# Two accumulators of the four-output stages from another PSUM pool, the first norm's factor later, the output in four stores

## The chip, the cores and the metric

One core of a Trainium2 chip runs the whole program. The metric is the device time of one execution in microseconds (us). The core has TensorE (PE in the profile, its weight loads PEld), VectorE (DVE), ScalarE (ACT), GpSimd (POOL) and SyncE (SP); a q behind the name is the engine's instruction queue, where waits and DMA issues stand.

## The reference

Two layers on 256 tokens of width 1024, in float32, batch 1:

```python
for l in range(DEPTH):                       # DEPTH = 2
    h = rms_norm(x, norm_mix_w[l])
    x = x + hybrid_mixer(h, ...)             # attention over 64 chosen keys + a Mamba-2 scan, gated, merged
    h = rms_norm(x, norm_ffn_w[l])
    x = x + conv_glu_ffn(h, ...)             # up to 2 x 2816, causal conv, silu gate, down
return rms_norm(x, norm_final_w)
```

`rms_norm` divides a token by the root of its mean square and multiplies by a weight. `hybrid_mixer` multiplies h by `w_in`: 584 columns with index queries, index keys and head weights, together with 32 columns of time steps, make the 616 "narrow columns"; then come q, k, v, the scan's columns and two gates. The results are projected, gated, added and multiplied by `w_out`.

## The kernel before

Activations stand transposed in SBUF: 8 tiles of 128 features by 256 tokens (`xT`). Every float32 product is made of three fp32r products: high part of the weights by high part of the input, high by low, low by high. The weights come in 512 KB chunks through SP's queue into 5 buffers (`raw`); ACT casts a chunk to its high part (`whi`, L199), DVE subtracts to get the low part (`wlo`, L200), into 3 pairs of buffers. Some chunks are split long ahead into SBUF tiles that are free just then (names with an e in front: `es`, `ez`, `ex`, `eths`, `eXt`, `ebig`, `ehxh`, `ehxl`). `take()` hands the next chunk to the products.

PSUM has 8 banks, each a tile: 4 with the tag `acc` (sums of the big products), 2 with `sa` (attention and half of the narrow columns), 2 with `sb` (norms and scan). Two helpers make the big products:

- `n_outer` makes one tile of 128 outputs, over all inputs, in one `acc` bank: 16 high products (L376, L377) and 8 low ones (L382) for each chunk.
- `k_outer` makes four tiles of outputs at once in four banks, input by input, so that it can start before its last inputs are there. There are four of these stages in a layer: the scan's projection (inputs `bH`), `w_out` (`mH`), FFN up (`uh`) and FFN down (`fH`). In each the four outputs come first and `n_outer` makes the others.

The tiles are emptied by DVE or ACT: `merge` (L841), `residual` (L857, adds to `xT`, then makes the next norm's inputs `uh`, `ul` and squares `sq`), `times_factor` (L891).

The norm's factor is not needed by the products: sums of squares collect in `ssq` on POOL (L343), `factor()` adds them over features with 8 small TensorE products against ones (L361), takes the power -0.5 on POOL (`ny`, L282), and, one step later, spreads it to a row (L289, L290, L298, L300). `factor()` is a side task: it is registered with a delay, counted in chunks taken, and its instructions are queued on TensorE behind the last low product emitted until then (`issue_after(st["mm"].ins)`).

```python
side("norm", nrm.factor(), 7)      # first norm of the program
side("norm", nrm.factor(), 2)      # in the w_out stage, for the FFN's norm
```

The first norm's factor so comes when the eighth and last narrow chunk (k = 7) is taken. The narrow columns take two `acc` and two `sa` banks; their eviction by ACT (L570 to L572) multiplies by the factor.

The order on each engine is not the program's: a planner replays it on modelled times and lays each engine's instructions out in a fixed order, in which each then waits for its semaphores. Weight splits, and the norm's steps after the small products, have high priority in it.

At the end four transposed tiles of the output (two halves `h` for each of two blocks of tokens `c`) are scaled by the last norm's factor, `h = 0` on ACT (L932), `h = 1` on DVE (L930), and each `c` is stored with one DMA on SP's queue (L933).

Of the kernel before, what the change touches and what calls it, by code (L numbers as in the profile page):

```python
# [18 lines left out]
P = 128  # L19
L = 2  # L20
T = 256
D = 1024
KD = D // P
# [40 lines left out]
def hybrid_kernel(ctx: ExitStack, tc: tile.TileContext, a: dict, out: bass.AP):  # L64
    nc = tc.nc
# [9 lines left out]
    def pst(tag, shape, bufs):  # L75
        t = psum.tile([P, 512], F32, name=tag, tag=tag, bufs=bufs)
        n = int(np.prod(shape[1:]))
        v = t[:shape[0], :n]
        if len(shape) == 3:
            v = v.rearrange("p (a b) -> p a b", a=shape[1])  # L80
        return v
# [61 lines left out]
    def side(lane, gen, delay):  # L143


        lanes[lane].append([st["now"] + delay, gen])

    def side_step(lane):
        q = lanes[lane]
        with tc.issue_after(st["mm"].ins):  # L150
            d = next(q[0][1], None)
        if d is None:
            q.pop(0)
        else:
            q[0][0] = st["now"] + d
# [32 lines left out]
    def take():  # L188
        i = st["cur"]
        with tc.high_priority():  # L190
            load_some()
            while st["prep"] < len(order):
                j = order[st["prep"]]
                if j not in early and sum(k not in early for k in splits) == SPLIT_BUFS:
                    break
                src, b, c = chunks[j]
                hi, lo = (t[:, :b * c] for t in split_tiles(j))
                r = raws.pop(j)
                nc.scalar.copy(out=hi, in_=r)  # L199
                nc.vector.tensor_sub(lo, r, hi.bitcast(F32))  # L200
                splits[j] = [t.rearrange("p (b c) -> p b c", b=b) for t in (hi, lo)]
                st["prep"] += 1
                load_some()
        st["cur"] += 1
        if st["mm"] is not None:
            side_steps()
        return splits.pop(i)
# [29 lines left out]
    def constants():  # L237
        with tc.issue_after(nrm.add.ins):
            nc.gpsimd.dma_start(ident, a["ident"])
            nc.gpsimd.dma_start(small[:, L * KD:], a["small"][:, L * KD:])  # L240
            nc.gpsimd.dma_start(tri, a["tri"])
            nc.gpsimd.dma_start(rope, a["rope"])
            nc.gpsimd.dma_start(cmask, a["cmask"])
        nc.vector.tensor_scalar(neg, cmask, -FILL, FILL, op0=OP.mult, op1=OP.add)
        nc.vector.tensor_scalar(half, small[:, o0:o0 + L * 5 * XT], 0.5, None, op0=OP.mult)

    def sm(name, l=None, n=None):
        o, w = _SMALL[name]
        v = small[:, o:o + w]
        if l is not None:  # L250
            v = v[:, l * (w // L):(l + 1) * (w // L)]
        return v
# [117 lines left out]
    def acc_tile():  # L370
        return pst("acc", [P, T], 4)

    def feed_high(ps, wh, hi, lo, ks, first):

        for j, k in enumerate(ks):
            nc.tensor.matmul(ps, wh[:, j, :], hi(k), start=first and j == 0, stop=False)  # L376
            nc.tensor.matmul(ps, wh[:, j, :], lo(k), start=False, stop=False)  # L377

    def feed_low(ps, wl, hi, ks, last):

        for j, k in enumerate(ks):
            st["mm"] = nc.tensor.matmul(ps, wl[:, j, :], hi(k), start=False, stop=last and j == len(ks) - 1)  # L382

    def k_outer(n_pairs, hi, lo):

        pss = [acc_tile() for _ in range(4)]
        for j in range(n_pairs):
            wh, wl = (w.rearrange("p (k n) c -> p k n c", k=2) for w in take())
            for kk in range(2):
                for n in range(4):  # L390
                    feed_high(pss[n], wh[:, kk, n:n + 1, :], hi, lo, [2 * j + kk], j == 0 and kk == 0)
            for n in range(4):
                feed_low(pss[n], wl[:, :, n, :], hi, [2 * j, 2 * j + 1], j == n_pairs - 1)
        return pss
# [9 lines left out]


    nrm = Normed(sm("nmw", 0))
    side("norm", nrm.factor(), 7)

    for l in range(L):

# [132 lines left out]
        def wide(pss, ws, hi, lo, first, last):  # L543

            halves = [slice(t * P, (t + 1) * P) for t in range(2)]
            for t, s in enumerate(halves):
                for ps, w in zip(pss[t], ws):
                    nc.tensor.matmul(ps, hi[:, s], w[0], start=first, stop=False)  # L548
            for t, s in enumerate(halves):
                for ps, w in zip(pss[t], ws):  # L550
                    nc.tensor.matmul(ps, lo[:, s], w[0], start=False, stop=False)  # L551
            for t, s in enumerate(halves):
                for ps, w in zip(pss[t], ws):
                    st["mm"] = nc.tensor.matmul(ps, hi[:, s], w[1], start=False, stop=last)  # L554

        pss = [[pst("acc", [P, 308], 4), pst("sa", [P, 308], 2)] for _ in range(2)]
        for k in range(KD):
            if l == 0:
                nrm.parts(k)
                for i in ([k - 1] if k < KD - 1 else [k - 1, k]):  # L560
                    if i >= 0:
                        nrm.square(i)
                if k == 3:
                    constants()
            wh, wl = take()
            ws = [(wh[:, 0, o:o + 308], wl[:, 0, o:o + 308]) for o in (0, 308)]
            wide(pss, ws, nrm.hi(k), nrm.lo(k), k == 0, k == KD - 1)
        for t in range(2):
            r = nrm.cols[:, t:t + 1]
            nc.scalar.activation(tok[t][:, 308:576], pss[t][1][:, 0:268], AF.Copy, scale=r)  # L570
            nc.scalar.activation(wd[:, t, :], pss[t][1][:, 268:308], AF.Copy, scale=r)
            nc.scalar.activation(tok[t][:, 0:308], pss[t][0], AF.Copy, scale=r)  # L572
# [3 lines left out]
        for c in range(2, 5):  # L576
            pss = [pst("acc", [P, 512], 4) for _ in range(2)]
# [6 lines left out]
            for t in range(2):  # L584
# [4 lines left out]
                else:  # L589
                    o = 576 + (c - 3) * 512  # L590
# [222 lines left out]
        for g in range(4):  # L813
            finish("scan", 3 - g)
            y = xs[g]
            for i in range(4):
# [6 lines left out]
                if i == 0:  # L823
                    acc = tmp.tile([P, T], F32, name="ssq", tag="ssq", bufs=3)
# [21 lines left out]
        for n, ps in enumerate(k_outer(8, bh, bl)):  # L846
            merge(n, ps)
# [6 lines left out]
        nrm = Normed(sm("nfw", l))  # L854
# [5 lines left out]
        for n, ps in enumerate(k_outer(4, mh, ml)):  # L860
            residual(n, ps, 0.5)
# [27 lines left out]
        def times_factor(ps):  # L889
            t = tmp.tile([P, T], F32, name="cu", tag="cu", bufs=4)  # L890
            nc.vector.tensor_mul(t, ps, nrm.row)  # L891
            return t

        pss = k_outer(4, nrm.hi, nrm.lo)
        finish("norm")
        us = [times_factor(ps) for ps in pss]
# [14 lines left out]
        nrm = Normed(sm("nlw") if last else sm("nmw", l + 1), not last)  # L911
# [9 lines left out]
    y = act.tile([P, 2, 2, 512], F32, name="y", tag="hxl")  # L921
    for c in range(2):
        for h in range(2):
            ps = pst("acc", [P, 512], 4)
            for i in range(4):
                nc.tensor.transpose(ps[:, i * P:(i + 1) * P], nrm.xw[:, 4 * h + i, c * P:(c + 1) * P], ident)
            o = y[:, c, h, :]
            r = nrm.cols[:, c:c + 1]
            if h:
                nc.vector.tensor_scalar(o, ps, r, None, op0=OP.mult)  # L930
            else:
                nc.scalar.activation(o, ps, AF.Copy, scale=r)  # L932
        nc.sync.dma_start(out[c * P:(c + 1) * P, :], y[:, c].rearrange("p a b -> p (a b)"))  # L933

# [81 lines left out]
```

## Time and profile before

| | |
|---|---|
| device time, 3 runs | 1081.49, 1083.02, 1076.52 us; median 1081.49 us |
| the profiled execution | 1080.03 us, its span 1078.2 us |
| granted TensorE clock, mean | 0.998 |
| PE, DVE, ACT, POOL busy | 1062.6, 862.8, 694.0, 81.7 us |
| TensorE products | 8713 |
| bytes moved by DMA | 191.84 MB, mean 178 GB/s |

The span runs from the first to the last instruction; 1.83 us of the execution's time lie around it. A product is shown from its issue to a modelled end, 0.28 us for 256 columns, although the next one starts 0.12 us later; so the busy time of TensorE is not its load, and an idle time shown before a product is 0.16 us shorter than the stop.

### The profile page before, as it was taken

The page shows a single profiled execution, that of the slowest core. Times are in us where ns is not written, and L with a number is a line of the kernel's source. Part 1 is how long each engine was busy: PE and PEld are TensorE (multiplying, and loading weights), DVE is VectorE, ACT ScalarE, POOL GpSimd, SP SyncE. Part 2 cuts the span into 40 slices and gives each one's busy share as a digit, 9 for nine tenths or more (in the row PEclk, how much of TensorE's full clock was granted, in tenths as well). Part 3 has the DMA queues.
Part 4 walks back from the last instruction along what each step waited for, and adds up shares of the span by engine and source line. Part 5 has one row for each costly group of instructions (what it writes and reads, how often), then busy time and mean ns, then how long its engine had stood idle before and what let it go on. Part 6 is the DMA issues. An engine that isn't in the chain of part 4 may idle for free.

```text
span 1078.2 us, 22404 instructions
## 1 busy us (share of the span) xinstructions
PE 1062.6 (99%) x8713; PEld 1023.9 (95%) x8713; DVE 862.8 (80%) x1652; ACT 694.0 (64%) x1285; POOL 81.7 (8%) x86
## 2 busy tenths in 40 slices
PE   8999999999999999999999999999999999999997
PEld 7789998999999999999997999999999999999997
DVE  6999987979776898886577999887895878988642
ACT  6758887657555566665455788875674555666552
POOL 3000000024000100000100000000420020000010
PEclk9999999999999999999999999999999999999999
DMA  8646544555677346667645654455567761666661
GB/s 303 189 149 206 156 157 145 168 167 179 193 238 238 102 138 196 195 190 232 186 136 175 218 167 126 164 165 161 178 181 220 247 213 40 195 195 192 187 182 50
DMA packets 53530, 191.84 MB, mean 178 GB/s; under 512 B 6144, under 2 KB 7184, under 8 KB 52400
## 3 DMA queue, kind: packets, MB, share of 16 engines
q1 hardware_dynamic: 51840, 181.23, 54.4%
q0 software_dynamic: 1440, 9.16, 2.3%
q8 instruction: 69, 1.13, 0.4%
q14 instruction: 37, 0.30, 0.1%
q10 hardware_dynamic: 144, 0.01, 0.0%
HBM read 189.26 MB, written 1.11 MB: 177 GB/s over the span
## 4 chain that ended last, share of the span: by engine, by line
PE 88%; DMA 4%; DVE 3%; issue 2%; ACT 2%; POOL 0%; SPq 0%; POOLq 0%; DVEq 0%; ACTq 0%
PE acc L376 24%; PE acc L377 24%; PE acc L382 24%; PE acc L551 2%; PE acc L554 2%; PE acc L548 2%; DMA raw<-in_wu_dram 2%; PE sb L729 1%; PE sa L613 1%; PE sa L465 1%; DVE wlo L200 1%; PE sa L638 1%; DMA bc<-prd 1%; DVE ul L330 1%; DMA raw<-in_wi_dram 1%
## 5 line engine op out<-in xcount | busy, mean ns | idle before, releaser
L199 ACT CAST whi<-raw 128x1024 fp32r<-128x1024 f32 (+2 forms) x320 | 331.9, 1041 | 227.6 <-PE acc L377 172.8
L200 DVE TENSOR_TENSOR wlo<-raw,whi 128x1024 fp32r<-128x1024 f32 (+2 forms) x320 | 387.4, 1213 | 102.7 <-ACT whi L199 96.0
L376 PE MATMUL acc<-hxh,whi 128*128 128x256 f32 x1456 | 352.5, 282 | 0.0
L377 PE MATMUL acc<-hxl,whi 128*128 128x256 f32 x1456 | 349.7, 280 | 0.0
L377 PEld LDWEIGHTS acc<-hxl,whi 128*128 128x128 f32 x1456 | 274.2, 188 | 2.3 <-issue 2.2
L376 PEld LDWEIGHTS acc<-hxh,whi 128*128 128x128 f32 x1456 | 274.2, 188 | 1.6 <-issue 1.5
L382 PE MATMUL acc<-hxh,wlo 128*128 128x256 f32 x1456 | 202.6, 280 | 0.0
L382 PEld LDWEIGHTS acc<-hxh,wlo 128*128 128x128 f32 x1456 | 182.7, 188 | 0.5 <-issue 0.3
L376 PE MATMUL acc<-fH,whi 128*128 128x256 f32 x352 | 84.4, 279 | 1.3 <-DVE xT L857 1.3
L377 PE MATMUL acc<-fL,whi 128*128 128x256 f32 x352 | 84.2, 279 | 0.0
L673 DVE SCALAR_TENSOR_TENSOR cv<-acc,half,cv 128x255 f32<-128x255 f32 (+2 forms) x144 | 66.9, 473 | 4.2 <-ACT cv L671 3.8
L875 DVE SCALAR_TENSOR_TENSOR cv<-acc,small,cv 128x255 f32<-128x255 f32 (+1 forms) x144 | 68.7, 477 | 1.4
L376 PEld LDWEIGHTS acc<-fH,whi 128*128 128x128 f32 x352 | 66.1, 188 | 1.6 <-issue 1.5
L343 POOL TENSOR_TENSOR ssq<-ssq,sq 128x256 f32<-128x256 f32 x30 | 28.3, 943 | 503.5 <-ACT sq L339 499.3
L377 PEld LDWEIGHTS acc<-fL,whi 128*128 128x128 f32 x352 | 66.0, 188 | 0.0
L376 PE MATMUL acc<-bH,whi 128*128 128x256 f32 x256 | 62.3, 280 | 0.0
L377 PE MATMUL acc<-bL,whi 128*128 128x256 f32 x256 | 62.2, 282 | 0.0
L382 PE MATMUL acc<-fH,wlo 128*128 128x256 f32 x352 | 49.6, 279 | 0.0
L376 PEld LDWEIGHTS acc<-bH,whi 128*128 128x128 f32 x256 | 48.1, 188 | 0.3 <-issue 0.2
L377 PEld LDWEIGHTS acc<-bL,whi 128*128 128x128 f32 x256 | 48.2, 188 | 0.0
L719 ACT ACTIVATE bc<-bc,nP 128x128 f32<-128x128 f32 x128 | 39.8, 391 | 10.3 <-DMA bc<-prd 10.2
L382 PEld LDWEIGHTS acc<-fH,wlo 128*128 128x128 f32 x352 | 44.8, 188 | 0.0
(312 smaller groups left out, 1848.9 us busy)
## 6 DMA issues: line engine op xcount, KB each, us to landing
raw<-in_wu_dram SPq DMA_DIRECT2D x88, 512.0 KB, 4.2
raw<-in_wx_dram SPq DMA_DIRECT2D x48, 512.0 KB, 3.7
raw<-in_wd_dram SPq DMA_DIRECT2D x38, 512.0 KB, 4.3
raw<-in_wz_dram SPq DMA_DIRECT2D x32, 512.0 KB, 3.6
raw<-in_wp_dram SPq DMA_DIRECT2D x32, 512.0 KB, 4.6
raw<-in_wq_dram SPq DMA_DIRECT2D x24, 512.0 KB, 4.3
raw<-in_wgs_dram SPq DMA_DIRECT2D x16, 512.0 KB, 3.6
bc<-prd POOLq DMA_DIRECT2D x8, 1024.0 KB, 7.4
```

The costliest lines, as they stand in the source:

```text
L199: nc.scalar.copy(out=hi, in_=r)
L200: nc.vector.tensor_sub(lo, r, hi.bitcast(F32))
L343: self.add = nc.gpsimd.tensor_add(self.acc, self.acc, sq)
L376: nc.tensor.matmul(ps, wh[:, j, :], hi(k), start=first and j == 0, stop=False)
L377: nc.tensor.matmul(ps, wh[:, j, :], lo(k), start=False, stop=False)
L382: st["mm"] = nc.tensor.matmul(ps, wl[:, j, :], hi(k), start=False, stop=last and j == len(ks) - 1)
L548: nc.tensor.matmul(ps, hi[:, s], w[0], start=first, stop=False)
L551: nc.tensor.matmul(ps, lo[:, s], w[0], start=False, stop=False)
L554: st["mm"] = nc.tensor.matmul(ps, hi[:, s], w[1], start=False, stop=last)
L673: nc.vector.scalar_tensor_tensor(v[:, j:], ps[:, :T - j], cw(l, 3 - j, i), v[:, j:], op0=OP.mult, op1=OP.add)
L719: nc.scalar.activation(E[:, h, :], E[:, h, :], AF.Relu, bias=nP[:, c, 8 * g + h:8 * g + h + 1])
L875: nc.vector.scalar_tensor_tensor(v[:, j:], uu[:, :T - j], fw(l, 2 - j, i), v[:, j:], op0=OP.mult, op1=OP.add)
```

## The change

`k_outer` takes two banks with the tag `acc` and two with `sa`, in that order, instead of four `acc`. The first norm's factor gets a delay of 9 chunks, which is not reached in the narrow stage; instead its first step is emitted right behind the stage's loop, in front of the evictions. Each block of the output is stored in two halves of 128 x 512 numbers, `h = 0` through SP's queue, `h = 1` through POOL's, each as soon as it is scaled.

```diff
     def k_outer(n_pairs, hi, lo):
 
-        pss = [acc_tile() for _ in range(4)]
+        pss = [pst(tag, [P, T], bufs) for tag, bufs in (("acc", 4), ("acc", 4), ("sa", 2), ("sa", 2))]
...
     nrm = Normed(sm("nmw", 0))
-    side("norm", nrm.factor(), 7)
+    side("norm", nrm.factor(), KD + 1)
...
             wide(pss, ws, nrm.hi(k), nrm.lo(k), k == 0, k == KD - 1)
+        if l == 0:
+            side_step("norm")
         for t in range(2):
...
                 nc.scalar.activation(o, ps, AF.Copy, scale=r)
-        nc.sync.dma_start(out[c * P:(c + 1) * P, :], y[:, c].rearrange("p a b -> p (a b)"))
+            (nc.gpsimd if h else nc.sync).dma_start(out[c * P:(c + 1) * P, h * 512:(h + 1) * 512], o)
```

## Rows read from the trace of the kernel before

**Rows 1.** The chain that ended last, shares of the span by engine.

```profile
PE 88%; DMA 4%; DVE 3%; issue 2%; ACT 2%; POOL 0%; SPq 0%; POOLq 0%; DVEq 0%; ACTq 0%
```

**Rows 2.** Waits of PE: waiting line, who ended it, total us, times, longest.

```profile
PE acc L376 <- DVE xT L857: 4.4, 5, 1.3
PE sb L361 <- POOL ssq L343: 1.5, 1, 1.5
...
PE acc L376 <- DVE cu L891: 0.4, 2, 0.2
```

**Rows 3.** Timeline of PE, narrow columns: start, us, instruction, count, [idle before].

```profile
19.83 0.38 PE L361 MATMUL sb<-ones,ssq 128*128 128x1 f32 x2 [1.49 <-POOL ssq L343]
...
20.75 0.38 PE L548 MATMUL sa<-eXt,uh 128*128 128x308 f32 x1
...
22.10 0.63 PE L548 MATMUL acc<-whi,uh 128*128 128x512 f32 x2
...
31.14 0.62 PE L548 MATMUL acc<-whi,uh 128*128 128x512 f32 x2
```

**Rows 4.** Timelines of POOL, DVE and ACT around the first factor.

```profile
18.02 1.76 POOL L343 TENSOR_TENSOR ssq<-ssq,sq 128x256 f32<-128x256 f32 x2 [3.51 <-ACT ea L513]
...
22.81 0.15 DVE L281 TENSOR_SCALAR nm<-sb 128x2 f32<-128x2 f32 x1
...
24.70 0.69 ACT L289 ACTIVATE dg<-ident,ny 128x128 fp32r<-128x128 f32 x2 [2.44 <-POOL ny L282]
...
27.18 1.07 ACT L199 CAST whi<-raw 128x1024 fp32r<-128x1024 f32 x1
```

**Rows 5.** Timeline of PE, layer 0, w_out to FFN up.

```profile
343.51 0.36 PE L376 MATMUL acc<-mH,whi 128*128 128x256 f32 x1 [0.18 <-DVE xT L857]
...
354.89 0.28 PE L376 MATMUL acc<-uh,es 128*128 128x256 f32 x1
...
356.45 0.39 PE L376 MATMUL acc<-uh,es 128*128 128x256 f32 x1 [0.93 <-DVE xT L857]
...
359.95 0.28 PE L361 MATMUL sb<-ones,sq 128*128 128x1 f32 x2
...
368.77 0.38 PE L376 MATMUL acc<-uh,ex 128*128 128x256 f32 x1 [0.21 <-DVE cu L891]
```

**Rows 6.** Timelines of ACT and DVE in the same stretch.

```profile
345.49 1.05 ACT L199 CAST es<-raw 128x1024 fp32r<-128x1024 f32 x1 [4.27 <-DMA raw<-in_wu_dram]
...
355.99 0.41 DVE L857 SCALAR_TENSOR_TENSOR xT<-acc,xT 128x256 f32<-128x256 f32 x1
...
359.20 0.40 ACT L339 ACTIVATE sq<-xT 128x256 f32<-128x256 f32 x1
```

**Rows 7.** Timelines of PE and ACT, the same place in layer 1.

```profile
872.22 0.36 PE L376 MATMUL acc<-mH,whi 128*128 128x256 f32 x1 [0.70 <-DVE xT L857]
...
885.08 0.38 PE L376 MATMUL acc<-uh,es 128*128 128x256 f32 x1 [1.27 <-DVE xT L857]
...
887.83 0.40 ACT L339 ACTIVATE sq<-xT 128x256 f32<-128x256 f32 x1
...
888.59 0.28 PE L361 MATMUL sb<-ones,sq 128*128 128x1 f32 x2
```

**Rows 8.** Timeline of PE, layer 0, FFN down.

```profile
509.94 0.36 PE L376 MATMUL acc<-fH,whi 128*128 128x256 f32 x1 [1.30 <-DVE xT L857]
```

**Rows 9.** The output's stores: SP's timeline, and GB/s in 40 slices of 1060 to 1079 us.

```profile
1073.28 0.34 SPq L933 DMA_DIRECT2D out_dram<-y  x1
...
GB/s 0 0 0 0 0 0 0 0 0 0 0 0 0 0 0 0 0 0 0 0 34 0 0 0 0 0 0 0 276 423 414 423 440 233 0 0 0 17 0 0
```

**Rows 10.** DMA issues by line: count, KB of each, us from issue to landing.

```profile
out_dram<-y SPq DMA_DIRECT2D x1, 512.0 KB, 3.2
...
prd<-pr POOLq DMA_DIRECT2D x1, 32.0 KB, 3.9
...
bc<-prd POOLq DMA_DIRECT2D x2, 1024.0 KB, 9.1
```

## The prediction

> **What bounds the kernel now.** I read the chain of waits first: 88% of the span lies on TensorE, the rest in small shares [rows 1]. So only two kinds of time can be won: stops of TensorE, and the ends of the span where it has nothing to do. The table of TensorE's own waits comes next, and it is short: 4.4 us for `residual`'s evictions, 0.4 us for `times_factor`'s, 1.5 us for the first norm's sum of squares [rows 2]. Each part of the change aims at one of these or at the tail. The shown idle time understates a stop by 0.16 us (a product is drawn 0.28 us long and issued every 0.12 us). The three stretches were then read as timelines, TensorE beside the engine that ends its wait.
>
> **Part 1: two accumulators from `sa`.** Before, the four outputs hold all four `acc` banks, and the next tile waits for the first eviction. After, two `acc` banks are free when the four outputs end, and when four outputs begin, the banks of the last two evictions are not needed. `sa` has no other user in these stages: attention is finished before the scan's projection, and the next layer's narrow columns come after four more tiles. No instruction is added or removed. The stops that should go, shown idle plus 0.16 each: layer 0, w_out's fifth tile 0.34, FFN up's third output 1.09, FFN up's next tile 0.37 [rows 5], FFN down's fifth tile 1.46 [rows 8]; layer 1, 0.86 and 1.43 at the same first two places [rows 7], and a second wait for `cu` as large as the first [rows 2], 0.37. Sum 5.9 us.
>
> But two of them don't stay won. Behind the first chunk of FFN up the FFN norm's small products are queued on TensorE, and the last of their inputs is the square of the eighth tile. In layer 0 that square ends at 359.20 + 0.40 = 359.60 and the product that reads it issues at 359.95 [rows 5, 6]: 0.35 us of slack. The square hangs on `residual` of the last tile, and DVE is late there by itself: ACT stood 4.27 us at the early split `es` for its DMA, and DVE works off splits and residuals from then on (the seventh tile's eviction starts at 355.99, 1.1 us after FFN up's first product at 354.89) [rows 5, 6]. TensorE's stops don't delay this chain, so their removal doesn't hasten it. If TensorE comes 0.34 + 1.09 = 1.43 us sooner with the same products queued ahead, it waits 1.1 us for the square: kept 0.33. In layer 1 the square ends at 888.23, its product issues at 888.59, slack 0.36 [rows 7]; of 0.86 + 1.43 = 2.29 us 1.96 is given back, kept 0.33. What waits behind that product on TensorE is the rest of FFN up. The other stops have nothing of the kind behind them: the next norm's small products come only after FFN down's last tile, whose eviction follows TensorE, and after `times_factor` the products are plain.
>
> I take that the small products keep their place, since the code ties them to the first chunk's last product and the planner can put them further back only by as much as its own modelled square is late. Part 1 then gives 0.33 + 0.37 + 1.46 in layer 0 and 0.33 + 0.37 in layer 1: 2.9 us, bounds 2.9 and 5.9.
>
> **Part 2: the first factor behind the narrow columns.** Before, its products are queued inside the products of k = 7, and TensorE stops 1.49 + 0.16 = 1.65 us for `ssq`; it then runs them until 20.75, and the nine products left of k = 7 until 22.10 [rows 3]. After, those nine (1.35 us) run while `ssq` is made. TensorE had stopped at 19.83 - 1.65 = 18.18, so it is through at 19.53, and POOL's sum ends at 18.02 + 1.76 = 19.78 [rows 4]; the factor still runs from 19.83 to 20.75, and the q, k, v stage starts 1.35 us sooner. The wait that is left, 0.3 us, has that stage queued behind it. The evictions and the row need the factor at the same time as before: it is made from the same sum at the same moment. The risk is DVE's queue: `nm` runs at 22.81 although its input is there at 20.75 [rows 3, 4], because splits are queued in front of it. If it falls behind one more split, ACT stands longer at `dg` (already 2.44 us), with the evictions and the next weight split (27.18) behind it. That split ends at 28.25 and TensorE wants it at 31.14, then 29.79 [rows 3, 4]: a shift of 1.2 us still fits. More than one split can't get in front, as the next one is itself behind `dg` on ACT. The attention's index steps start from these evictions and meet TensorE 1.35 us earlier in its queue; their slack isn't shown by one row. So between 0 and 1.35; I take 1.0, near the row's own arithmetic, less something for those steps.
>
> **Part 3: four stores on two queues.** Before, the second store issues at 1073.28 and lands 3.2 us later, 1076.5; the bytes run at 414 to 440 GB/s nearly throughout [rows 9, 10]. The same megabyte still has to pass. SP's halves need only ACT's copies, which saves at most 0.1 us at their start, and bounds the gain. POOL's last half needs DVE's second copy, as the second store did, so it issues at 1073.3. No row shows a store of 256 KB from POOL. Nearest is `prd`, 32 KB, 3.9 us [rows 10]: landing 1077.2, 0.7 us later than now. Its queue shared the DMA engines with weights, and here with 0.75 MB of the same stores; I take 0.4 us lost, bounds -0.1 and +0.7. [...]
>
> **Sum.** 2.9 + 1.0 - 0.4 = 3.5 us from the profiled 1080.03: 1076.5. The profiled execution lies 1.5 below the median of the three runs, and they spread over 6.5 us; I forecast 1077.0 for the median of the changed kernel, between 1076.5 and 1081.49 - 3.5 = 1078.0. Below 1% (10.8 us) faster or slower can't be told from no change for this kernel, and no sum of these parts comes near it.
>
> **The rivals.**
>
> *Small products move back.* If the planner lays the FFN norm's products behind more of FFN up in both layers, nothing takes the place of the removed stops: part 1 gives 5.9, with part 2 at 1.35 and the tail at 0.1 it is 7.4, time 1072.7. For it: the planner knows nothing of the DMA wait that makes `es` late, against it: then it also sees no reason to wait. Chance 0.2.
>
> *The time is given back.* After the start the feeding engines, DVE above all (862.8 us busy of 1078.2), set the pace of the first attention, and TensorE meets late index steps; or the planner's new order makes new waits of the size of the old. Then parts 1 and 2 leave 0 to 2 us, and the tail takes 0.4: about 1079.5. For it: DVE's delay of `nm` and the 0.35 us of slack show how near the feeders are. Against it: TensorE has no other wait of size in its table [rows 2]. Chance 0.19.
>
> *The change doesn't do what it says.* If `sa` isn't free when four outputs begin, the stops stay where they were under another name; only part 2 and the tail remain, 1079.4. The code leaves no user; chance 0.03.
>
> *POOL's store sets the end.* It decides as soon as POOL's last half lands later than 3.2 us after its issue, and from 3.2 + 3.9 = 7.1 us on the whole is slower than before. `bc` on this queue took 9.1 us in the median of two, for four times the bytes with weights beside it [rows 10]; at that it lands 9.1 - 3.2 = 5.9 us later against its issue than the store of before, and the time is 1080.03 - 3.9 + 5.9 = 1082.0. Against it: at the end nothing but these stores uses the engines. Chance 0.06.
>
> **How the numbers follow.** The forecast has 0.5, the rivals 0.2, 0.19, 0.03 and 0.06, and 0.02 are for what I didn't think of. The range takes in the first rival's 1072.7 less the runs' scatter and reaches to the last one: 1071.5 to 1082.0; under 0.2 is left outside. Faster by over 1% would need more than all parts at their best, or a new order from the planner that helps elsewhere: 0.06. Slower by over 1% needs a bad one: 0.06. Within 1%: 0.88.
>
> **What would show it.** Part 1: no wait of L376 for `xT` or `cu` in TensorE's table, FFN down's fifth tile following at the pace; and in their place a wait of L361 for ACT's `sq`, 1.1 us in layer 0 and 2.0 in layer 1. If that wait is missing, the first rival holds. Part 2: L361 waits 0.3 us for `ssq`, and the first 512-column product at 20.75 instead of 22.10; `nm` still at or near 22.8. Part 3: POOL's second half is the last to land, 3.6 us after its issue, SP's second half before it. What would make the prediction wrong: an order of the planner that moves more than the four places named, or a POOL store as slow as `bc`.

## The result and the profile after

The changed kernel takes **1068.95 us** (median of 4 runs, 1067.94 to 1073.08) against 1081.89 us for the kernel before (median of 4, the three runs above and one more). The ratio is 0.9875, with a 95% interval of 0.9838 to 0.9912: 1.25% faster. The prediction was 1077.0 us with a range from 1071.5, so the change brought about 13 us where 3.5 were forecast. Two further measurements of the changed kernel, beside other experiments, gave 0.9884 [0.9851, 0.9917] and 0.9882 [0.9855, 0.9909].

The profiled execution took 1067.94 us with a span of 1066.1, 12.1 us less than before's 1078.2. Behind the narrow columns' stage the line numbers are 2 higher: L857 is L859, L891 is L893, L933 is L935. First the chain that ended last, as [rows 1], then the waits of TensorE, as [rows 2]:

```profile
PE 87%; DMA 6%; DVE 3%; issue 1%; ACT 1%; POOL 0%; SPq 0%; POOLq 0%; DVEq 0%; ACTq 0%
```

```profile
engine line waited for: us in total, times, longest us
PE sb L225 <- DVE ones L213: 1.3, 1, 1.3
PE sb L361 <- POOL ssq L343: 1.0, 2, 0.7
PE acc L548 <- ACT whi L199: 0.3, 1, 0.3
PE sb L361 <- ACT sq L339: 0.3, 2, 0.2
```

The waits for `xT` (4.4 us) and `cu` (0.4 us) are gone. In their place stand four waits of the FFN norm's small products, two in a layer. They are where the prediction put its give-back: the rows of layer 0, then layer 1, answer to [rows 5, 7].

```profile
351.40 0.38 PE L361 MATMUL sb<-ones,ssq 128*128 128x1 f32 x2 [0.65 <-POOL ssq L343]
...
352.87 0.38 PE L361 MATMUL sb<-ones,sq 128*128 128x1 f32 x2 [0.15 <-ACT sq L339]
...
876.23 0.38 PE L361 MATMUL sb<-ones,ssq 128*128 128x1 f32 x2 [0.38 <-POOL ssq L343]
...
877.70 0.38 PE L361 MATMUL sb<-ones,sq 128*128 128x1 f32 x2 [0.15 <-ACT sq L339]
```

With 0.16 us for each wait's drawn end, that is 1.12 us in layer 0 (predicted 1.1) and 0.85 us in layer 1 (predicted 1.96).

So the waits explain part of the 12.1 us, and not most of it. To find the rest, the n-th large product of TensorE in one trace was set against the n-th in the other, 7872 in each. The table gives how much earlier each kernel is than before at the same product (us; worked out from the starts in the traces; "part 1 alone" and "part 2 alone" are experiments below):

| place (its time before) | changed | part 1 alone | part 2 alone |
|---|---|---|---|
| first large product (5.7) | 0.39 | -0.36 | -0.57 |
| attention of layer 0 begun (112.2) | 4.48 | -1.95 | 3.58 |
| scan of layer 0 (239.8) | 6.44 | -1.02 | 5.58 |
| before w_out ends (336.6) | 6.71 | -0.74 | 5.76 |
| FFN up begun (375.0) | 7.49 | 0.56 | 6.00 |
| FFN down begins (500.3) | 7.49 | 0.56 | 6.00 |
| layer 1 begins (541.1) | 9.75 | 2.83 | 6.21 |
| layer 1, before w_out ends (836.8) | 9.72 | 2.79 | 6.16 |
| FFN up of layer 1 begun (911.1) | 11.13 | 4.84 | 6.23 |
| FFN down of layer 1 begins (1024.9) | 11.14 | 4.84 | 6.23 |
| last product (1068.2) | 12.02 | 5.72 | 6.86 |

The largest step is the first, 4.1 us up to 112 us, and the stop that was removed there had been only 1.65 us long. The narrow columns after, against [rows 3]: the small products follow the last products of k = 7, and the first 512-column product issues at 20.32 in place of 22.10. The second view is POOL's, the sum of squares, against [rows 4].

```profile
19.37 0.30 PE L554 MATMUL sa<-epT,uh 128*128 128x308 f32 x1
19.51 0.28 PE L361 MATMUL sb<-ones,ssq 128*128 128x1 f32 x2
...
20.32 0.71 PE L548 MATMUL acc<-whi,uh 128*128 128x512 f32 x2
```

```profile
17.36 1.79 POOL L343 TENSOR_TENSOR ssq<-ssq,sq 128x256 f32<-128x256 f32 x2 [2.80 <-ACT ea L513]
```

That is the factor, 1.8 us: the whole stop is gone, as the sum ends at 19.15 here (17.36 + 1.79) and TensorE comes for it at 19.51. (The earlier start of 0.4 us is no part of it: it was lost again in the first 16 us, and the last products in front of the old stop stand within 0.1 us of before's.) The rest, 2.7 us between 39 and 112 us, comes from a line that nothing in the diff touches: the index scores (L465, shown as `64*128`: 64 active rows for each product; the even heads' slice is rows 0 to 63, the odd heads' rows 64 to 127). TensorE's timeline in layer 0, before:

```profile
46.52 0.71 PE L465 MATMUL sa<-kk,qiT 64*128 64x128 f32 x4
48.52 0.71 PE L465 MATMUL sa<-kk,qiT 64*128 64x128 f32 x4
52.79 1.13 PE L465 MATMUL sa<-kk,qiT 64*128 64x256 f32 x4
54.51 1.13 PE L465 MATMUL sa<-kk,qiT 64*128 64x256 f32 x4
```

after, in layer 0:

```profile
46.88 0.71 PE L465 MATMUL sa<-kk,qiT 64*128 64x128 f32 x8
52.07 1.13 PE L465 MATMUL sa<-kk,qiT 64*128 64x256 f32 x8
57.91 1.14 PE L465 MATMUL sa<-kk,qiT 64*128 64x256 f32 x8
```

and before once more, in layer 1:

```profile
575.14 0.72 PE L465 MATMUL sa<-kk,qiT 64*128 64x128 f32 x8
586.65 1.13 PE L465 MATMUL sa<-kk,qiT 64*128 64x256 f32 x8
```

Eight products take the time of four. Before, layer 1 had them in eights and layer 0 in fours; after, both layers have eights. The planner, replaying other times behind the moved factor, laid the order out anew. The groups of this line show the whole, before and then after (busy us, mean ns of one):

```profile
L465 PE MATMUL sa<-kk,qiT 64*128 64x256 f32 x32 | 6.8, 402 | 0.0
L465 PE MATMUL sa<-kk,qiT 64*128 64x128 f32 x32 | 4.3, 297 | 0.0
```

```profile
L465 PE MATMUL sa<-kk,qiT 64*128 64x256 f32 x32 | 4.5, 402 | 0.0
L465 PE MATMUL sa<-kk,qiT 64*128 64x128 f32 x32 | 2.9, 297 | 0.0
```

11.1 us became 7.4 us with the same 64 products of the same mean length. From each product's start to the next one's, which is what TensorE's queue feels, it is 10.20 and 6.84 us: 3.36 us, nearly as much as the whole forecast. The table shows only 2.7 us of it up to 112 us because the new order also draws six attention products in front of this place that stood behind it; the table's next step, up to 240 us, is larger for it.

### The profile page after: what moved, and what is told of

Same layout as the page of the kernel before. It is cut to its first block, busy times and chain, and to the rows that moved or that the text cites. A ratio compares the mean times of both kernels' runs of the same rounds, so it can differ in the third digit from the quotient of the medians.

```text
span 1066.1 us, 22377 instructions
## 1 busy us (share of the span) xinstructions
PE 1056.1 (99%) x8713; PEld 1020.8 (96%) x8713; DVE 860.7 (81%) x1652; ACT 694.8 (65%) x1285; POOL 81.4 (8%) x88
## 4 chain that ended last, share of the span: by engine, by line
PE 87%; DMA 6%; DVE 3%; issue 1%; ACT 1%; POOL 0%; SPq 0%; POOLq 0%; DVEq 0%; ACTq 0%
PE acc L376 22%; PE acc L377 22%; PE acc L382 22%; DMA raw<-in_wu_dram 5%; PE acc L548 3%; PE acc L551 3%; PE acc L554 3%; PE sa L377 2%; PE sa L376 2%; PE sa L382 2%; PE sb L731 2%; DVE ul L330 1%; PE sa L615 1%; PE sa L640 1%; DVE wlo L200 1%
## 5 line engine op out<-in xcount | busy, mean ns | idle before, releaser
L343 POOL TENSOR_TENSOR ssq<-ssq,sq 128x256 f32<-128x256 f32 x30 | 27.8, 928 | 498.4 <-ACT sq L339 495.1
L376 PE MATMUL acc<-fH,whi 128*128 128x256 f32 x264 | 64.0, 277 | 0.0
L377 PE MATMUL acc<-fL,whi 128*128 128x256 f32 x264 | 63.9, 277 | 0.0
L377 PEld LDWEIGHTS acc<-fL,whi 128*128 128x128 f32 x264 | 49.6, 188 | 0.0
L376 PEld LDWEIGHTS acc<-fH,whi 128*128 128x128 f32 x264 | 49.5, 188 | 0.0
L377 PE MATMUL acc<-bL,whi 128*128 128x256 f32 x192 | 47.6, 282 | 0.0
L376 PE MATMUL acc<-bH,whi 128*128 128x256 f32 x192 | 47.5, 279 | 0.0
L830 POOL TENSOR_TENSOR ssq<-ssq,sq 128x256 f32<-128x256 f32 x24 | 32.2, 1343 | 136.5 <-ACT sq L829 136.1
L875 ACT ACTIVATE cv<-acc,small 128x256 f32<-128x256 f32 x72 | 40.6, 563 | 0.1
L382 PE MATMUL acc<-fH,wlo 128*128 128x256 f32 x264 | 37.8, 277 | 0.0
L377 PEld LDWEIGHTS acc<-bL,whi 128*128 128x128 f32 x192 | 36.2, 188 | 0.0
```

What stands on the lines that cost most here:

```text
L830: nc.gpsimd.tensor_add(acc, acc, sq)
L875: nc.scalar.activation(v, uu, AF.Identity, scale=fw(l, 2, i), bias=fb(l, i))
```

## The experiments

All ratios are against the kernel before, run beside the experiment, with a 95% interval.

### The three parts alone

Part 1 is `pss = [pst(tag, [P, T], bufs) for tag, bufs in (("acc", 4), ("acc", 4), ("sa", 2), ("sa", 2))]` alone; part 2 the delay `KD + 1` and `side_step("norm")` alone; part 3 the four stores alone.

> Only the first part: two accumulators of the four-output stages from the other pool. Theory A (each part brings what its own stretch of the two traces shows): from the scan's projection on, TensorE's products come 5.6 us sooner by the last one (0.3 scan's projection, 0.8 w_out and FFN up of layer 0, 1.5 FFN down, 0.1 and 1.3 in layer 1, and 1.6 from the closer spacing of products in the last four tiles of both FFN downs), the first 200 us are as before, and the whole is 5 to 6 us faster. The prediction on record: 2.9 us, with TensorE waiting 1.1 and 2.0 us for the squares of the FFN norms. Rival B (the gain hangs on the new order as a whole): under 2 us or over 8 us.

Part 1: 1073.08 us, ratio 0.9924 [0.9895, 0.9954]. Its waits of TensorE:

```profile
PE sb L361 <- POOL ssq L343: 1.3, 1, 1.3
PE sb L225 <- DVE ones L213: 1.3, 1, 1.3
PE acc L548 <- ACT whi L199: 0.9, 1, 0.9
PE sb L361 <- ACT sq L339: 0.3, 2, 0.2
```

No `xT` or `cu`, and the 1.3 us is the first norm's old stop. In the table it loses 1.6 us up to 112 us, before its own edit acts: a spell at a lower clock behind that stop (0.57 from 22.5 to 25.5 us, last section). Its 0.9 us wait at `whi` stands ahead of the first large product and isn't in these 1.6 us. From there on it gains 7.7 us: 0.93 up to 240 us, 0.28 up to w_out, 1.30 around w_out and FFN up, 2.27 at FFN down, 2.05 and 0.88 at the same places of layer 1. The index scores stay at 10.20 us. By the times part 1 is worth 8.2 us (the ratio) to 9.8 us (the medians), more than the 5 to 6 expected, so they don't rule out the rival's bound of 8 us; the trace has the gain at the places that were named.

> Only the second part: the first norm's factor behind the narrow columns. Theory A: 6.0 us faster, all of it before 220 us: 1.3 from the stop inside the narrow columns, 3.3 because the index scores of layer 0 stand in groups of eight instruction halves on TensorE, both halves of its rows at work together, and the rest from small stops (one of 0.8 us in the scan). Behind 220 us nothing changes. The prediction on record: 1.0 us (bounds 0 and 1.35). Rival B: about 1.3 us, the earlier products of the changed kernel having come from somewhere else.

Part 2: 1076.91 us, ratio 0.9943 [0.9921, 0.9965]. It gains 6.2 us from its first product to 240 us and then 1.3 us more in all; the index scores take 6.84 us. Up to the scan's projection its order on TensorE is that of the changed kernel.

> Only the third part: the output in four stores on two queues. Theory A: within 0.3 us of before, as the tail of the changed kernel is 0.1 us shorter; last landing no later than before. The prediction on record: 0.4 us slower, POOL's second half landing last, 3.6 us after its issue. Rival C (more queues start the bytes sooner): over 0.5 us faster.

Part 3: 1085.4 us, ratio 1.0022 [0.9995, 1.0049]. From the start of the last product to the end of the span it takes 7.37 us, against 7.46 before: 0.1 us better. Its span of 1082.6 us is longer for another reason, told in the last section.

The three ratios multiplied give 0.9889 (0.9924 x 0.9943 x 1.0022), near the 0.9875 of the whole: within the intervals the parts add up.

### What the score products gain from

> The kernel before, with nothing of the change; instead the eight index-score products of a step are queued behind two products of two columns, one into each of their two banks, so that the products of both row halves stand together in layer 0 as they did in layer 1. Theory A (halves that stand together run at the same time): the scores of layer 0 take half the time, 2.5 to 3.4 us less, the 16 small products cost about 1 us, and the whole is 1 to 3 us faster. Rival D (the scores of layer 0 were slow for another reason, such as the banks' eviction by ACT): they take as long as before, and the whole is 0 to 2 us slower.

```diff
+                free = [nc.tensor.matmul(ps[:, 0, 0:2], ones_r, ones_r[:, 0:2], start=True, stop=True) for ps in pss]
+                with tc.issue_after(free[0].ins), tc.issue_after(free[1].ins):
                     for i in range(2):
                         for e in range(2):
```

1082.38 us, ratio 0.9998 [0.9977, 1.0020]. The score products did move together (6.8 and 4.3 us became 4.5 and 3.3), and the total didn't move. Up to 112 us the scores' stretch took 1.7 us less, where the changed order brought 2.7. The gain was lost again to longer stops, 1.5 us at `bt` (0.6 before) and 2.0 us at FFN down (1.3 before), and to a lower clock at 22.5 us (0.53) and behind FFN down's stop (0.57 from 509 to 513 us). The run shows that pairs can be forced and, for the whole, not what they are worth.

So the changed kernel was taken as it is, and only the rows were changed, which leaves every engine's order the same, but for the places of single score products within their groups of eight:

```diff
-                        hs = slice(e * 64, (e + 1) * 64)
+                        hs = slice(0, 64)
```

> The changed kernel, but the index scores of the odd heads read the same 64 rows of TensorE as the even heads (the slice is 0 to 64 for both; so the scores of the odd heads are left out and those of the even ones made twice). The order of instructions on every engine is the same as in the changed kernel. Theory: the score products of the two halves run at once, since they use different rows of TensorE, where the planner puts them together; that is what the new order of layer 0 gained (10.20 to 6.84 us for all score products). On the same rows they have to run one after the other, in both layers: the score products take 13.4 us or more, and the time is about 6.6 us above the changed kernel's, 1075.5, between 1074.5 and 1077. Rival: the gain came from the new order's having fewer changes between shapes of products, not from two running at once; then rows don't matter, the score products stay at 6.8 us, and the time is 1069 within 0.5.

1074.09 us, against 1068.19 for the changed kernel beside it: 5.9 us more, just under the expected range, as the score products took 12.6 us and not 13.4. The same groups of eight, and their sum:

```profile
47.19 1.16 PE L465 MATMUL sa<-kk,qiT 64*128 64x128 f32 x8
52.82 1.99 PE L465 MATMUL sa<-kk,qiT 64*128 64x256 f32 x8
```

```profile
L465 PE MATMUL sa<-kk,qiT 64*128 64x256 f32 x32 | 8.0, 389 | 0.0
L465 PE MATMUL sa<-kk,qiT 64*128 64x128 f32 x32 | 4.6, 285 | 0.0
```

On the same rows the eight take 1.99 us and not 1.13. So two of these products do run at once, on different rows, when they are neighbours in the queue. The starts in the traces show it directly, for 256 columns: in the changed kernel the two products of a pair start at most 14 ns apart and the inner pairs follow each other every 216 ns; on the same rows, and in layer 0 before, single products follow each other every 216 ns.

The rival is refuted as the main cause but holds a part. From start to start the scores of layer 0 take 6.78 us before, 6.01 on the same rows and 3.42 in the changed kernel. So of 3.36 us 2.6 come from running at once, and 0.8 from two groups of four becoming one of eight: of a group's products on the same rows the first takes 320 ns to the next start, the last 306, those between 216. TensorE's large products confirm the first part: behind the scores of each layer they come 2.5 to 2.6 us later than in the changed kernel. What makes a group's ends longer, 320 and 306 ns against 216, no run shows.

### What the small products' waits are worth

The FFN norm's factor one chunk later in the changed kernel, run twice, the second time beside the changed kernel:

```diff
-        side("norm", nrm.factor(), 2)
+        side("norm", nrm.factor(), 3)
```

> The changed kernel with the FFN norm's factor one chunk later (delay 3 in place of 2 in the w_out stage, both layers); nothing else is changed. What I hold now: in the changed kernel TensorE stops at the small products of that norm (0.81 + 0.32 us shown in layer 0, 0.55 + 0.32 us in layer 1), and this is all that is left of part 1's give-back; one chunk later the sums are there, the four waits vanish, and the time is 1067.0 (1068.95 less 2.0), between 1066.8 and 1068.2. Rival 1: the spread factor then comes late for the first eviction of FFN up (times_factor), and TensorE waits for cu instead, 0.4 to 1.5 us in a layer: time 1068 to 1070. Rival 2, my prediction's view that the feeding chain alone sets the pace there: what is won at the small products is lost at the next product of FFN up that hangs on the same chain, time 1069 within 0.5.

> The changed kernel with the FFN norm's factor one chunk later, a second time, beside the changed kernel itself. Its first look had the four waits of the small products gone (layer 0 1.35 us sooner, layer 1 1.07 us), but FFN up of layer 0 ran at 117.7 ns a product and not at 113.3, and the median came to 1071.1. If the pace is chance and not the program's, this median comes near 1068.2 less 2 = 1066.2 whenever FFN up is at the fast pace, its times fall into groups near 1066.5 and 1071, and about as many of them are in the upper group as for the changed kernel (1 or 2 of 6). Rival: the later factor itself brings the slow pace; then 4 or more of 6 are near 1071 again.

> The changed kernel a third time, as the comparison for the kernel before it in this call. Median 1068.5 within 1; times in two groups, near 1068 and near 1072, the upper with 1 or 2 of 6.

1071.12 us (0.9900 [0.9864, 0.9936]) and 1071.46 us (0.9907 [0.9877, 0.9936]), against 1068.63 us (0.9882) for the changed kernel. The second profile of the edit, which is its fastest run (1066.52 us, span 1064.7), has these waits of TensorE and no others:

```profile
PE sb L225 <- DVE ones L213: 1.3, 1, 1.3
PE acc L548 <- ACT whi L199: 0.3, 1, 0.3
PE sb L761 <- ACT bt L751: 0.2, 1, 0.2
```

The four waits are gone and nothing took their place there: against the first profile of the changed kernel, TensorE gains 1.2 us in layer 0 and 1.1 in layer 1 around FFN up's first products. The causes that the two rivals of the first expectation name aren't in the trace. But both medians miss the expected 1066.8 to 1068.2, and 9 of its 12 runs lie above 1069 us, against 4 of 12 of the changed kernel beside them, though its best runs are the fastest of all (1066.5). The edit's first profile (1071.13 us) ran FFN up of layer 0 at the slower of two paces, told below, which took 3.5 us. The rival of the second expectation, that the later factor itself brings this pace more often, has the numbers on its side, but they are few, and the profile of the kernel with one store a block, below, has the slower pace in this place without the later factor. Why the pace differs is open.

### The stores, and the changed kernel again

> The changed kernel with part 3 undone (one store for each block of tokens on SP's queue, as before); the order on TensorE, DVE and ACT is the same. The prediction's price for part 3: it loses 0.4 us, so this kernel is 0.4 us faster than the changed one, and its tail, from the start of TensorE's last product to the end of the span, is 0.4 us shorter than the changed kernel's. What the run of part 3 alone suggests: the tail is 0.1 us longer here, and the median within 0.3 us of 1068.95. Rival: the two queues save a whole landing, over 0.7 us.

1068.61 us (0.9891 [0.9856, 0.9926]) with one store a block, 1068.19 with four: no difference that these runs can tell. The tail is 7.46 us against 7.35 and 7.37. The stores of the changed kernel, as [rows 9, 10]:

```profile
1060.49 0.92 SPq L935 DMA_DIRECT2D out_dram<-y  x2
```

```profile
1060.83 1.20 POOL L935 DMA_DIRECT2D out_dram<-y  x2 [1.08 <-DVE y L932]
```

```profile
out_dram<-y SPq DMA_DIRECT2D x2, 256.0 KB, 2.0
out_dram<-y POOLq DMA_DIRECT2D x2, 256.0 KB, 3.0
```

POOL's halves do land last, 3.0 us after their issue, where I had taken 3.6.

> The changed kernel again, without an edit, beside the three others on the same chip, to compare them with. Theory on the two paces: the step from product to product, 113.3 or 117.7 ns for 256 columns at a granted clock of 1.00, belongs to the execution and not to the program; then in this profile other stretches are at the slow pace than in the first profile of the changed kernel, and the count of products at the slow pace (3641 there) differs by hundreds, each hundred 0.44 us of the span. Rival: the pace belongs to the program's place or data; then the same stretches are slow, and the count is within 100 of 3641. The median is 1069 within 1 in either case.

1068.19 us (0.9884). The profile has 3658 products at the slower pace, 3641 in the first: within 100, so this run alone speaks for the rival. The two profiles of the later factor, in the last section, speak against it.

## Why the prediction was wrong

**Part 2 is the step that failed.** I took 1.0, between 0 and 1.35, because I moved the factor inside an order of TensorE that I held fixed, and asked only whether the attention's steps would come late. The stop itself gave 1.8 us and not 1.35, since POOL's sum came sooner than the 19.78 I had taken and left no wait (0 to 0.3 us in the eight profiles with part 2). The larger miss is another: the move changed the planner's times, and the new order put the scores' halves side by side. That is 3.4 us, which part 2 alone has too, and 2.6 of which the same rows take back. The second rival feared a new order, and 0.06 stood for "a new order from the planner that helps elsewhere", without a price. The trace of before held the price: layer 1 had the same line in eights, layer 0 in fours.

Some of the table's step from 112 to 240 us is chance: the profile of before has a stop there that the changed kernel's hasn't, and parts 1 and 3 alone, which don't touch this stretch, were also 0.9 us quicker through it; the kernel with one store a block, in the changed order, has the stop again (0.59 us shown). TensorE's timeline, before:

```profile
184.48 1.12 PE L759 MATMUL sb<-Xd,bt 128*128 128x512 f32 x2 [0.64 <-ACT bt L749]
```

**Part 1 was sized too small.** In layer 0 the numbers came out: from w_out to FFN up the gain is 0.78 us (forecast 0.70), the give-back 1.12 (forecast 1.1), and FFN down's stop gave 1.46 us (1.46). In layer 1 the gain is 1.41 and not 0.70. The step that failed, in both layers, is "TensorE's stops don't delay this chain, so their removal doesn't hasten it". The chain starts where ACT gets the load for the split `es`. ACT after, in layer 0 (against [rows 6]) and layer 1, and then before in layer 1:

```profile
337.12 1.05 ACT L199 CAST es<-raw 128x1024 fp32r<-128x1024 f32 x1 [3.15 <-DMA raw<-in_wu_dram]
...
861.95 1.05 ACT L199 CAST es<-raw 128x1024 fp32r<-128x1024 f32 x1 [2.87 <-DMA raw<-in_wu_dram]
```

```profile
874.12 1.05 ACT L199 CAST es<-raw 128x1024 fp32r<-128x1024 f32 x1 [4.20 <-DMA raw<-in_wu_dram]
```

The split starts 8.37 us earlier in layer 0 (345.49 - 337.12) and 12.17 in layer 1 (874.12 - 861.95), where the table's lead on the way in is 6.71 and 9.72: 1.7 and 2.5 us sooner than TensorE. But the first four evictions, which DVE had done while it waited for this split, now stand behind it. DVE in layer 0, before (its own half of the split starts at 346.57) and after (at 338.20; the other two evictions, from `sa`, follow):

```profile
342.95 1.41 DVE L857 SCALAR_TENSOR_TENSOR xT<-acc,xT 128x256 f32<-128x256 f32 x4
```

```profile
339.34 0.75 DVE L859 SCALAR_TENSOR_TENSOR xT<-acc,xT 128x256 f32<-128x256 f32 x2
```

So the way from ACT's split to the last square takes 15.3 us in all eight profiled executions with part 1 and 13.7 in the four without it, in both layers. ACT's last squares after, layer 0 and layer 1, against [rows 6, 7]:

```profile
352.42 0.40 ACT L339 ACTIVATE sq<-xT 128x256 f32<-128x256 f32 x1
```

```profile
877.24 0.40 ACT L339 ACTIVATE sq<-xT 128x256 f32<-128x256 f32 x1
```

In layer 0 that is 6.78 us earlier (359.20 - 352.42) at a lead of 6.71: the two changes, 1.7 and 1.6 us, cancel, so the forecast was right there by luck. In layer 1 it is 10.59 us earlier (887.83 - 877.24) at a lead of 9.72: 0.9 us sooner, so that 0.85 and not 1.96 us was given back. Measured in this way, the split is 1.6 to 2.2 us ahead in layer 0 and 2.4 to 3.1 us in layer 1 in the eight profiles with part 1; in the three others besides before's it is 0 to 0.5 us, once 1.3. So part 1 does hasten the load that this chain starts from. Whether the removed stops do it or the new order of splits and loads is not shown.

The remainder, 0.8 and 0.9 us in the two FFN down stages, is in the main a change of pace (last section; 0.7 us in each by the share of products at either pace). All eight profiled executions with part 1 have the quicker pace in both of these stages (16 of 16), the four without it in 4 of 8. That is in its favour; I know no reason, and count it as open.

**Part 3 was sized with the wrong sign.** -0.4 was taken, and the tail measured +0.1. `prd`'s 3.9 us was the wrong neighbour: the same 32 KB took 1.75 us in layer 0 and 3.93 us in layer 1 of the changed kernel's profile. That the weights beside it make the difference is argued, not shown. For POOL's 256 KB stores the trace has 3.0 us and no loss of the tail.

The sum that the profiles give for 12.1 us, rounded: the start -0.1; the factor's stop 1.8; the scores 3.4; the rest up to 240 us 1.3, of which 0.9 are the stop at `bt`; part 1's places 0.3 (the scan's projection), 0.8 and 1.4 (w_out and FFN up of the two layers) and 1.5 (FFN down's stop); the rest of the two FFN down stages 0.8 and 0.9; the tail 0.1. The stop at `bt` is this pair of profiles and not the change; the 0.3 may be in part, as parts 2 and 3 alone gain 0.1 to 0.2 us there too.

Of the rivals, "the small products move back" didn't happen, though doing it by hand showed that its mechanism is real. "The time is given back", "doesn't do what it says" and "POOL's store sets the end" are refuted by the waits and the tail.

## What to carry to other kernels

Where a planner lays out each engine's order, an edit's price has two terms, the stop it removes and the order that it causes; the second can be the larger (here 3.4 us against 1.8), and only a trace of the new order shows it. Before pricing such an edit, compare the same line in two layers or passes of the old trace: equal work at unequal time is what a new order can win or lose. And where a group of products uses half of TensorE's rows, look whether its other half stands next to it in the queue (2.6 us here).

## What the runs showed of the hardware

**Two paces at one clock.** Products of 256 columns follow each other every 113.3 or every 117.7 ns (mean shown length 276 or 281 ns), over hundreds of products, at the same granted clock of 1.00. The pace goes with the place: the scan's projection runs at the slower one nearly throughout in all twelve profiles, and of their 24 FFN up stages 20 run at the quicker one. But in some places one program can show both. The same stretch of FFN up, the same program (factor one chunk later), two executions, the second profile first; then one line from 382 to 476 us in the kernel before and with the stores alone, whose order on TensorE is the same:

```profile
core 0: us, PE busy (x) PEld busy (x) DVE busy (x) ACT busy (x) POOL busy (x), PEclk, DMA share, GB/s
386.00:472.00 86.00, 86.00 (x760) 86.00 (x760) 78.48 (x132) 59.49 (x99) 0.00 (x0) 1.00 0.66 195
```

```profile
386.00:472.00 86.00, 86.00 (x732) 86.00 (x732) 75.69 (x128) 58.17 (x94) 0.00 (x0) 1.00 0.64 186
```

```profile
L376 PE MATMUL acc<-hxh,whi 128*128 128x256 f32 x276 | 64.3, 276 | 0.0
```

```profile
L376 PE MATMUL acc<-hxh,whi 128*128 128x256 f32 x268 | 64.7, 281 | 0.0
```

760 against 732 products in 86 us. Over FFN up of one layer this is 3.8 us. The profile of the stores alone had it in both layers, 7.6 us, more than the 4.4 us by which its span is longer than before's; the first profile of the later factor and the kernel with one store a block had it in layer 0. That a good part of the scatter of these kernels (5.1 us between the four runs of the changed kernel above) comes from it is my estimate from these 3.8 us. What sets the pace is open.

**A stop can cost more than its length.** With part 1 alone, TensorE ran at a granted clock of 0.57 behind the first norm's stop, 11 products in 3 us where the kernel before, with a stop of the same kind, had 16 behind it:

```profile
22.50:25.50 3.00, 3.00 (x11) 0.57 0.76 254
```

```profile
22.10:25.10 3.00, 3.00 (x16) 1.00 0.71 231
```

The same happened behind the small products' waits of FFN up in one of three profiles of the changed kernel, 0.54, and in the one with one store a block. In the former, 16 products of 256 columns follow each other every 213 ns in this stretch:

```profile
355.70:359.40 3.70, 3.70 (x21) 0.54 0.48 152
```

For most of these stretches, behind a stop, the products stood 1.8 to 1.9 times as far apart as usual, at a cost of 1.6 us with part 1 alone (six 308-column products at some 255 ns where 141 are usual, then four 512-column products at 427 ns and one at 321, where the next ones take 228) and of 1.5 us in FFN up (16 times 213 - 117.7 ns). In none of the eight profiles with part 2 did it come at the first norm, in two of the four without it it did.
